# The first mixer in a fixed order by hand, with its gate summed by products

## The chip, the core and the metric

One Trainium2 chip; the kernel runs on one of its cores. The engines meant below: PE (matrix products; PEld is its weight load), DVE (vector work), ACT (activations and casts), POOL, and SP, which issues the loads. The time is device microseconds (us) of one execution; lower is better. The kernel before takes 1494.75 us in the median of three runs (1491.81 to 1494.77).

## The reference, cut to what matters

Two blocks of a transformer over 256 tokens of width 1024, batch 1, all in fp32. The change touches the mixer of the first block:

```python
mod = c_act @ w_ada + b_ada          # conditioning: 6 vectors of 1024
sh1, sc1, g1, sh2, sc2, g2 = split(mod)
h = x * (1 + sc1) + sh1
q, k, v, qi, ki, wi, gate_b, gate_c, hc = split(h @ w_in)
q, k, qi, ki = partial_rope(...)     # 8 heads of 64, k and v shared; 8 index heads of 32
rel = relu(einsum('bqhd,bsd->bqhs', qi, ki))
score = einsum('bqhs,bqh->bqs', rel, wi)       # causal
sel = top_k(score, 64)               # each query keeps 64 keys
attn = group_rms_norm(softmax(q k / 8 over sel) @ v, g)
u = gate_c * hc
conv = sum(conv_w[j] * u_pad[:, j:j + s] for j in range(3))
conv_out = group_rms_norm(gate_b * conv, g)
mix = concatenate([attn, conv_out]) @ w_out
x = layer_norm(ALPHA * x + g1 * mix, ln1_g, ln1_b)
```

After it come the first swiglu ffn (with sh2, sc2, g2) and a second block with four ffns, a differential attention and a gated recurrence; they are as before in both kernels.

## The kernel before, in words

Tokens are two tiles t of 128 rows. A product of two fp32 operands is done as three on values cut into a high and a low part (hi x hi, hi x lo, lo x hi). For weights ACT casts a loaded piece to its high part (L210, `whi`) and DVE subtracts it to get the low one (L223, `wlo`). `Stream` (`W`) holds that for all weights in order: `load_to` issues a load on SP, `highs_to` the casts, `split_to` the subtractions, `next` hands a piece of two halves over. Loaded pieces lie in five buffers `raw`, which the weights share with the loads of the conditioning matrix (`adaraw`, 1 MB each like a weight piece); a load starts when the buffer that it takes is free.

The conditioning vectors that follow the mixer (G1 its gate, SH2 and SC2 shift and scale of the ffn) are made from four loads each. DVE multiplies a loaded row block by the conditioning value of its partition and adds it to `adacc`, two operations a load (L558 the first, L560 the others). PE then sums `adacc` over partitions: for a gate by two products with ones, which leave the sum in all rows (L580), for a shift or scale by eight one-column products (L605); DVE adds the bias (`vcol`, L607).

`first_mixer` modulates and projects (`ps_att`, k loop over eight blocks of the width, with a third of the first two conv products `ps_c` in it), then the indexer (`ps_idx` L1271, relu on ACT, `score` L1277, eight rounds of MAX8 and MATCH_REPLACE8 for each tile, L1289 and L1291, then the mask `mb`), then eight attention units (tile t, four heads `quad`, parity e: logits `ps_lg` L1323, masked minimum L1333, exp L1337, transposes `ps_pt` L1345, weighted sum L1355), the head norm and its split into `mh`, `ml`. The other two conv products `ps_c` and two gate products `ps_gb` run in pieces between, followed by the taps (L1155, L1157), `gated` (L1163), a group norm `ps_gn` (L1440 to L1452) and the split of those features. `ps_wo` is the product with w_out; `finish` adds its last pieces, calls `between`, and does the residual (`u`, L261) and the norm.

What sets the order there: `order(False)` hands the mixer to a scheduler that takes the instructions by priority, and the table PLACES gives units, fills, splits, sums and norms their ranks. The rest of the kernel runs `order(True)`, as written.

Of the kernel before, what the change touches and what calls it, by code (L numbers as in the profile page):

```python
# [9 lines left out]
F32 = mybir.dt.float32  # L10
# [21 lines left out]

PLACES = {
# [7 lines left out]
}  # L41
# [383 lines left out]
class Net:  # L425
    def __init__(self, nc, tc, T, out, ctx, stop=None):
# [18 lines left out]
        self.ada_seq = [u for j in range(4) for u in (columns[2 * j], (G1, j), columns[2 * j + 1])]  # L445
# [7 lines left out]
        W.add([T["w_out"][j] for j in (2, 3, 0, 1)])  # L453
# [556 lines left out]
    def first_mixer(self):  # L1010
        nc, T, tc, W = self.nc, self.T, self.tc, self.W
        with ExitStack() as es:
# [3 lines left out]
            self.gate_bounds()  # L1016
            rope = m1.tile([P, 2, 32], F32, name="rope")
# [68 lines left out]
            def prepared(k):  # L1086

                if k == KT:
                    W.split_to(2 * W.at + 1)
# [15 lines left out]
            for k in range(KT):  # L1105
                W.load_to(k + 2)
                load(k + 3)
                if k == KT - 3:
                    nc.sync.dma_start(out=self.blk64, in_=T["k_blk64"])
                    nc.sync.dma_start(out=rope, in_=T["k_rope"])  # L1110
                    nc.sync.dma_start(out=causal, in_=T["k_causal"])
# [9 lines left out]
                if k != KT - 2:  # L1121
                    while thirds:
                        conv_third(*thirds.pop(0))
                parts = coming

            self.order(False)
            rank0 = tc.cur_priority

            def rank(name, default):

                n = PLACES.get(name, default)
                return tc.high_priority(offset=tc.cur_priority - rank0 - n)

            urgent = lambda: rank("chain", 0)

            late = []
            cw = self.col("conv_w")
            cv = m1.tile([P, 4, S], F32, name="cv", tag="cv")
# [4 lines left out]
            def some(n):  # L1143
                while late and n:
                    late.pop(0)()
                    n -= 1

            def conv_in(j, ps):
                with rank(f"cv{j}", 100 + 10 * j):
                    gc = self.w256("gc")  # L1150
                    u = m2.tile([P, S + 2], F32, name="cu")
                    nc.gpsimd.memset(u[:, 0:2], 0.0)
                    nc.scalar.copy(gc, ps[:, :S])
                    nc.vector.tensor_tensor(out=u[:, 2:], in0=ps[:, S:], in1=gc, op=ALU.mult)
                    nc.vector.tensor_scalar(out=cv[:, j], in0=u[:, 0:S], scalar1=cw[:, j:j + 1], scalar2=None, op0=ALU.mult)  # L1155
                    for d in (1, 2):
                        nc.vector.scalar_tensor_tensor(out=cv[:, j], in0=u[:, d:d + S], scalar=cw[:, 4 * d + j:4 * d + j + 1],  # L1157
                                                       in1=cv[:, j], op0=ALU.mult, op1=ALU.add)

            def gated(j, ps):  # L1160
                with rank(f"gb{j}", 200 + 10 * j):
                    y = cv[:, 2 * j:2 * j + 2].rearrange("p a b -> p (a b)")
                    nc.vector.tensor_tensor(out=y, in0=ps, in1=y, op=ALU.mult)  # L1163
                    sq = m2.tile([P, 2, 512], F32, name="gsq", tag="gsq")
                    nc.scalar.activation(sq[:, 0], y, AF.Square)
                    ys.append((y, sq))

            def normed(j):
                y, sq = ys[j]
                with rank(f"gn{j}", 220 + 10 * j):  # L1170
                    r = self.group_rstd(m1, sq, self.eps1)

                def rest():
                    with rank(f"nr{j}", 220 + 10 * j):
                        for a in range(2):
                            f = 4 + 2 * j + a
                            hf = self.w256("hfc")
                            g = m2.tile([P, 1], F32, name="cg")
                            nc.vector.tensor_scalar(out=g, in0=self.col("conv_g", 2 * j + a), scalar1=-0.5, scalar2=None, op0=ALU.mult)
                            nc.vector.scalar_tensor_tensor(out=hf, in0=y[:, a * S:(a + 1) * S], scalar=g, in1=r()[:, a * S:(a + 1) * S],  # L1180
                                                           op0=ALU.mult, op1=ALU.mult)
                            self.split(mh[:, f], ml[:, f], hf)
                return rest

            def product(name, q, done):
                with rank(f"split{q}", 500 + 50 * q):
                    parts = W.next(ahead=0, ada=False)
                ps = self.psum("acc", name)
                for n in range(2):
                    pieces = self.feat_pieces(ps, parts, n * S, n * P)  # L1190
                    for piece in range(2):
                        with rank(f"fill{q}", 500 + 50 * q):
                            next(pieces)
                        if n and piece:
                            done(ps)
                        yield

            def work():
                for j in (2, 3):
                    yield from product("ps_c", j - 2, lambda ps, j=j: late.append(lambda: conv_in(j, ps)))  # L1200
                for j in range(2):
                    yield from product("ps_gb", j + 2, lambda ps, j=j: late.append(lambda: gated(j, ps)))
                while len(ys) < 2:
                    some(1)
                rests = [normed(0), normed(1)]
                for j, r in enumerate(rests):
                    r()
                self.out_acc = self.rows_acc("ps_wo")
                for q, ks in ((4, (4, 5)), (5, (6, 7))):
                    with rank(f"split{q}", 500 + 50 * q):  # L1210
                        parts = W.next(ahead=0, ada=False)
                    for a, k in enumerate(ks):
                        for t in range(2):
                            with rank(f"fill{q}", 500 + 50 * q):
                                self.rows_mm(self.out_acc[t], parts[a], t, lhs(k), k == 4, False)
                            yield

            ys = []
            fill = work()
            filled = lambda n: [next(fill, None) for i in range(n)]  # L1220

            with urgent():

                pj = [m1.tile([P, 1024], F32, name=f"pj{t}", tag=f"pj{t}")[:, :ATT_COLS] for t in range(2)]
                for t in range(2):
                    nc.scalar.copy(pj[t][:, 512:], acc[t][1][:, :ATT_COLS - 512])
                for t in range(2):
                    nc.scalar.copy(pj[t][:, :512], acc[t][0])

                def rot(t, base, heads, dim):  # L1230
                    v = pj[t][:, base:base + heads * dim].rearrange("p (h d) -> p h d", h=heads)
                    c2 = rope[:, t:t + 1, 0:16].to_broadcast([P, heads, 16])
                    s2 = rope[:, t:t + 1, 16:32].to_broadcast([P, heads, 16])
                    sw = m2.tile([P, 9, 16], F32, name="sw")[:, :heads]
                    nc.vector.tensor_tensor(out=sw[:, :, 0:8], in0=v[:, :, 8:16], in1=s2[:, :, 0:8], op=ALU.mult)
                    nc.vector.tensor_tensor(out=sw[:, :, 8:16], in0=v[:, :, 0:8], in1=s2[:, :, 8:16], op=ALU.mult)
# [24 lines left out]
            for j in range(2):  # L1261
                conv_in(j, pcs[j])
# [600 lines left out]
```

## Time and profile before

| | before |
|---|---|
| time, median of 3 runs | 1494.75 us |
| lowest and highest | 1491.81, 1494.77 us |
| the profiled execution: time, span | 1493.31 us, 1491.5 us |
| PE busy | 1412.9 us (95%) |
| DVE busy | 1117.4 us (75%) |
| ACT busy | 720.1 us (48%) |
| POOL busy | 46.0 us (3%) |

The span is what the trace covers; the 1.8 us beside it belong to the execution's start and end. Busy shares are of the whole span; the mixer ends near 180 us of it.

### The profile page before, as it was taken

Reading aid. Unit: us, or ns where it says so; the run is one execution under the profiler, and the core shown is the slowest. Engines: PE = TensorE matmul, PEld = TensorE weight load, DVE = VectorE, ACT = ScalarE, POOL = GpSimd, SP = SyncE. Lnnn points to the kernel's source line nnn. Section 1 sums busy time; section 2 is a strip of 40 time slices with the busy share of each in tenths; the row PEclk is TensorE's granted clock in tenths of the full one; section 3 lists DMA queues with packets and bytes.
Section 4 is the critical chain, followed back from the end, with each engine's and each line's share of the span. In section 5 each row is a group of like instructions: output and inputs, shape, how many; then the busy total and the mean of one; then the engine's idle time right before and its main releaser. Section 6 shows DMA issues by size and latency. Waiting matters only on the chain.

```text
span 1491.5 us, 22826 instructions
## 1 busy us (share of the span) xinstructions
PE 1412.9 (95%) x9218; PEld 1270.9 (85%) x9218; DVE 1117.4 (75%) x1742; ACT 720.1 (48%) x1218; POOL 46.0 (3%) x45
## 2 busy tenths in 40 slices
PE   6987898999899999899999999999999899999998
PEld 5965787999799989677799998999997888799997
DVE  5877877876888867888886667876666998766545
ACT  5544343434443445556454445544445675544343
POOL 0001000000000000122100000000000000000000
PEclk9967999999999999999999999999999999999999
DMA  8925567878467878476567676486654334356650
GB/s 323 342 91 194 212 243 287 288 286 316 150 229 303 351 301 297 185 255 207 189 235 262 259 271 230 175 319 245 245 213 156 114 114 151 132 198 244 239 181 29
DMA packets 50346, 337.87 MB, mean 227 GB/s; under 512 B 5648, under 2 KB 7440, under 8 KB 11200
## 3 DMA queue, kind: packets, MB, share of 16 engines
q1 hardware_dynamic: 50096, 336.35, 61.2%
q8 instruction: 72, 1.18, 0.3%
q14 instruction: 34, 0.28, 0.1%
q10 hardware_dynamic: 144, 0.07, 0.0%
HBM read 335.33 MB, written 1.06 MB: 226 GB/s over the span
## 4 chain that ended last, share of the span: by engine, by line
PE 75%; DVE 14%; ACT 4%; issue 3%; POOL 2%; DMA 1%; SPq 0%; POOLq 0%; DVEq 0%; ACTq 0%
PE ps_dn L699 19%; PE ps_up L663 12%; PE ps_up L661 12%; PE ps_up L660 12%; DVE wlo L223 3%; PE ps_up L853 2%; DVE adacc L560 2%; PE ps_att L699 2%; PE ps_wo L699 1%; POOL qss L637 1%; PE ps_up L860 1%; ACT whi L210 1%; PE ps_do L699 1%; PE ps_g L699 1%; POOL oss L637 1%
## 5 line engine op out<-in xcount | busy, mean ns | idle before, releaser
L223 DVE TENSOR_TENSOR wlo<-raw,whi 128x1024 fp32r<-128x1024 f32 (+2 forms) x429 | 502.6, 1208 | 52.1 <-ACT whi L210 51.8
L210 ACT CAST whi<-raw 128x1024 fp32r<-128x1024 f32 (+2 forms) x429 | 427.8, 1038 | 138.7 <-issue 47.8
L661 PE MATMUL ps_up<-xh,wlo 128*128 128x256 f32 x1600 | 392.3, 283 | 3.8 <-DVE wlo L223 3.8
L660 PE MATMUL ps_up<-xh,whi 128*128 128x256 f32 x1600 | 393.6, 284 | 0.4 <-ACT whi L210 0.4
L661 PEld LDWEIGHTS ps_up<-xh,wlo 128*128 128x128 f32 x1600 | 306.1, 191 | 7.0 <-DVE wlo L223 4.4
L660 PEld LDWEIGHTS ps_up<-xh,whi 128*128 128x128 f32 x1600 | 305.8, 191 | 3.9 <-ACT g L950 0.9
L663 PE MATMUL ps_up<-xl,whi 128*128 128x256 f32 x1600 | 224.4, 283 | 0.0
L663 PEld LDWEIGHTS ps_up<-xl,whi 128*128 128x128 f32 x1600 | 206.2, 192 | 0.0
L560 DVE SCALAR_TENSOR_TENSOR adacc<-adaraw,cact,adacc 128x1024 f32<-128x1024 f32 x154 | 196.8, 1281 | 2.4
L950 ACT ACTIVATE g<-ps_up 128x256 f32<-128x256 f32 x100 | 38.5, 385 | 315.8 <-PE ps_up L663 315.8
L699 PE MATMUL ps_dn<-whi,hh 128*128 128x512 f32 x440 | 173.9, 395 | 0.0
L699 PE MATMUL ps_dn<-wlo,hh 128*128 128x512 f32 x440 | 172.8, 393 | 0.6 <-DVE wlo L223 0.6
L952 DVE TENSOR_TENSOR hu<-ps_up,g 128x256 f32<-128x256 f32 x100 | 42.3, 423 | 153.2 <-ACT g L950 153.0
L699 PE MATMUL ps_dn<-whi,hl 128*128 128x512 f32 x440 | 140.7, 394 | 0.0
L699 PEld LDWEIGHTS ps_dn<-whi,hl 128*128 128x128 f32 x440 | 82.6, 188 | 18.6
L699 PEld LDWEIGHTS ps_dn<-wlo,hh 128*128 128x128 f32 x440 | 82.8, 188 | 18.2 <-DVE wlo L223 1.0
L699 PEld LDWEIGHTS ps_dn<-whi,hh 128*128 128x128 f32 x440 | 83.1, 189 | 17.0 <-issue 0.2
L644 DVE TENSOR_TENSOR hl<-hu,hh 128x256 fp32r<-128x256 f32 x100 | 42.5, 425 | 47.3 <-ACT hh L643 47.3
L643 ACT CAST hh<-hu 128x256 fp32r<-128x256 f32 x100 | 40.7, 407 | 72.3 <-DVE hu L952 72.3
L637 POOL TENSOR_TENSOR rstd<-rstd,mhalf 128x1 f32<-128x1 f32 x16 | 8.7, 546 | 892.0 <-DVE rstd L313 642.1
L379 ACT ACTIVATE xh<-ps_tr,vcol,modA 128x128 fp32r<-128x128 f32 x48 | 18.1, 457 | 31.0 <-PE ps_tr L368 25.6
L1768 PE MATMUL ps_l<-hX 128*128 128x128 f32 x224 | 29.8, 276 | 0.6 <-DVE hX L1753 0.6
(357 smaller groups left out, 1947.9 us busy)
## 6 DMA issues: line engine op xcount, KB each, us to landing
raw<-in_up_dram SPq DMA_DIRECT2D x110, 1024.0 KB, 6.4
adaraw<-in_ada_dram SPq DMA_DIRECT2D x88, 1024.0 KB, 5.2
raw<-in_down_dram SPq DMA_DIRECT2D x55, 1024.0 KB, 6.6
adas<-in_ada_s_dram SPq DMA_DIRECT2D x8, 1024.0 KB, 5.4
raw<-in_w_qk_dram SPq DMA_DIRECT2D x8, 1024.0 KB, 7.2
raw<-in_w_att_dram SPq DMA_DIRECT2D x8, 724.0 KB, 6.6
raw<-in_w_conv_dram SPq DMA_DIRECT2D x4, 1024.0 KB, 8.0
raw<-in_w_out_dram SPq DMA_DIRECT2D x4, 1024.0 KB, 5.9
```

The source lines that it names most:

```text
L210: net.nc.scalar.copy(hi[:, :n], src)
L223: self.net.nc.vector.tensor_tensor(out=lo[:, :n], in0=src, in1=hi.bitcast(F32)[:, :n], op=ALU.subtract)
L560: nc.vector.scalar_tensor_tensor(out=acc, in0=raw[:, k], scalar=c[:, 2 * j + k:2 * j + k + 1], in1=acc, op0=ALU.mult, op1=ALU.add)
L637: self.nc.gpsimd.tensor_tensor(out=out, in0=in_, in1=self.mhalf[:, :n], op=ALU.pow)
L643: nc.scalar.copy(hi, src)
L644: nc.vector.tensor_tensor(out=lo, in0=src, in1=hi.bitcast(F32), op=ALU.subtract)
L660: mm(o, hi[:, at(k)], xh[:, k], start=k == 0, stop=False)
L661: mm(o, lo[:, at(k)], xh[:, k], start=False, stop=False)
L663: mm(o, parts[k // 4][0][:, at(k)], xl[:, k], start=False, stop=k == KT - 1)
L699: mm = lambda *args, **more: self.nc.tensor.matmul(*args, **more, **kw)
L950: self.last_silu = nc.scalar.activation(g, ps[:, :S], AF.Silu)
L952: nc.vector.tensor_tensor(out=u, in0=ps[:, S:], in1=g, op=ALU.mult)
```

## The change

The scheduler and its table go: `order(True)` holds for the whole mixer, and a sequence written by hand takes the place of the ranks. The first token tile goes ahead through rotation, indexer, scores and top-8 rounds; the eight units are pipelined (unit i's logits beside the weighted sum of unit i-2 and the transposes of i-1), and `filled(n)` puts n steps of `fills()` between them. G1 is no longer summed on DVE: `cb` holds the conditioning vector copied into 128 columns, and 16 fp32 products of the loaded rows with it give the gate in all rows at once. So G1's four loads come first, in the last two rounds of the projection. The products c2, c3, gb0 and gb1 come in six steps of eight products each. The first tap and the gains of the heads are on ACT (`scalar`), the taps wait until the units end, w_out is used in its own order (attention features first), the second tile's head split moves ahead of `between`, and `summed()` does DVE's two sums of one load. The group norm takes another PSUM pool and buffer.

```diff
-PLACES = {
-    "ada0": -54, "ada1": -129, "ada10": 1501, "ada11": 1295, "ada2": 1040, "ada3": 585, "ada4": 957,
...
-        self.ada_seq = [u for j in range(4) for u in (columns[2 * j], (G1, j), columns[2 * j + 1])]
+        self.ada_seq = [(G1, j) for j in range(4)] + columns
...
-        W.add([T["w_out"][j] for j in (2, 3, 0, 1)])
+        W.add(T["w_out"])
...
+            cb = m1.tile([P, KT, P], F32, name="cb", tag="cv")
+            nc.vector.tensor_copy(cb, self.cact[:, :KT, None].to_broadcast([P, KT, P]))
...
-                W.load_to(k + 2)
+                W.load_to(min(k + 2, KT - 1))
                 load(k + 3)
+                if k >= KT - 2:
+                    self.ada_load()
+                    self.ada_load()
...
-            self.order(False)
-            rank0 = tc.cur_priority
...
+            def sums():
+
+                pss = [self.psum("acc", "ps_gate") for a in range(2)]
+                for j in range(4):
+                    raw = self.ada_raw.pop(j)
+                    for k in range(2):
                         for a in range(2):
+                            nc.tensor.matmul(pss[a], cb[:, 2 * j + k], raw[:, k, a * 512:(a + 1) * 512], start=j == k == 0, stop=j == 3 and k == 1)
+                            yield
+                got["gate"] = pss
...
+            def fills():
+                yield from sums()
+                for name in ("ps_c2", "ps_c3", "ps_gb0", "ps_gb1"):
+                    yield from product(name)
...
+            for i in range(8):
+                logits(i)
+                if i == 4:
+                    chosen(1, 2)
+                    masked(1)
+                least(i)
+                if i >= 2:
+                    weighted(i - 2)
+                if i >= 1:
+                    turned(i - 1)
+                weights(i)
...
+                if i == 7:
+                    W.split_to(c2 + 3)
+                    filled(3)
+
+            weighted(6)
+            turned(7)
+            head_split(0)
+            conv_in(2, got.pop("ps_c2"))
+            filled(1)
+            weighted(7)
+            W.highs_to(c2 + 5)
+            rest[1] = head_norms(1)
...
+            ys = [gated(0)]
+            W.highs_to(c2 + 9)
+            summed()
+            W.split_to(c2 + 8)
+            filled(3)
+            norms.append(self.group_rstd(m1, ys[0][1], self.eps1))
...
+            normed(1, ys[1][0], norms[1]())
+            W.split_to(c2 + 11)
+            parts = W.next(ahead=0, loads=0, ada=False)
+            wo = [(p, k) for k, p in enumerate(parts, 2)]
+            W.load_to(c2 // 2 + 7)
+            self.ada_load()
+            self.ada_load()
+            summed()
+            for t in range(2):
+                for p, k in wo:
+                    self.rows_mm(out[t], p, t, lhs(k), False, False)
+            summed()
+            self.ada_load()
+
             def between():
-                head_split(1)
-                self.reduce_now(G1)
                 self.reduce_sums(SH2, "b")
                 self.reduce_sums(SC2, "t")
...
-            self.finish(self.out_acc, lhs, range(4), End(self, G1, 1.0, nxt, None, "ln"), between=between)
+            self.finish(out, lhs, range(4, 8), End(self, G1, 1.0, nxt, None, "ln"), between=between)
...
+            if scalar:
+                nc.scalar.activation(hf[:, k], src, AF.Copy, scale=gains[k])
+            else:
+                nc.vector.tensor_scalar(out=hf[:, k], in0=src, scalar1=gains[k], scalar2=None, op0=ALU.mult)
```

On PE the indexer products stand so in the kernel before (`ps_idx` the indexer, `ps_c` a conv product; the numbers of columns at the end):

```order
L675 MATMUL ps_c<-xl,whi 128x256
L1271 MATMUL ps_idx<-kiT,qiT 128x256
L1271 MATMUL ps_idx<-kiT,qiT 128x128
L1271 MATMUL ps_idx<-kiT,qiT 128x256
L1271 MATMUL ps_idx<-kiT,qiT 128x128
L673 MATMUL ps_c<-xh,whi 128x256
```

And so in the changed kernel, from the indexer to the first units (`ps_gate` the new sums, `ps_q` and `ps_k` the transposes for the heads):

```order
L1271 MATMUL ps_idx<-kiT,qiT 128x256 x4
L1172 MATMUL ps_gate<-adaraw,cb 128x512 x2
L1271 MATMUL ps_idx<-kiT,qiT 128x256 x4
L1172 MATMUL ps_gate<-adaraw,cb 128x512
L1257 MATMUL ps_q<-ident,pj_631 128x128 x4
L1260 MATMUL ps_k<-ident,kr_701 128x128
L1257 MATMUL ps_q<-ident,pj_632 128x128 x4
L1260 MATMUL ps_k<-ident,kr_708 128x128
L1172 MATMUL ps_gate<-adaraw,cb 128x512 x2
L1314 MATMUL ps_lg<-kT,qT 128x128 x2
```

The conv pieces have left the indexer and the first units, the gate sums stand in their place, and four indexer products in a row now belong to one tile and four heads, on different row strips.

On DVE the end of the mixer stands so before (L560 the sums, L223 the low parts, L1433 the second head split, L607 the reduced vectors, L261 the residual):

```order
L560 SCALAR_TENSOR_TENSOR adacc<-adaraw,cact,adacc 128x1024 x3
L223 TENSOR_TENSOR wlo<-raw,whi 128x1024 x4
L1430 TENSOR_SCALAR hf<-ps_at,cols 128x128 x4
L1433 TENSOR_TENSOR ml<-hf,mh 128x4x128
L589 TENSOR_TENSOR gate<-ps_red,gate 128x512 x2
L607 TENSOR_TENSOR vcol<-ps_red,cols 128x8 x2
L223 TENSOR_TENSOR wlo<-raw,whi 128x1024
```

And in the changed kernel (all line numbers ten lower, L550 and L548 the sums, L213 the low parts, L597 the reduced vectors):

```order
L213 TENSOR_TENSOR wlo<-raw,whi 128x1024
L550 SCALAR_TENSOR_TENSOR adacc<-adaraw,cact,adacc 128x1024 x4
L213 TENSOR_TENSOR wlo<-raw,whi 128x1024 x5
L597 TENSOR_TENSOR vcol<-ps_red,cols 128x8
L548 TENSOR_SCALAR adacc<-adaraw,cact 128x1024
L550 SCALAR_TENSOR_TENSOR adacc<-adaraw,cact,adacc 128x1024 x7
L597 TENSOR_TENSOR vcol<-ps_red,cols 128x8
L213 TENSOR_TENSOR wlo<-raw,whi 128x1024
```

All eight sums of SC2 now stand behind five splits, the fifth of which is the first ffn weight's, and behind SH2's reduced vector; the head split and the gate's additions have gone from here.

## Rows read from the trace of the kernel before

**Rows 1.** Stretches of the mixer: length, busy us of each engine, granted clock, DMA share, GB/s.

```profile
core 0: us, PE busy (x) PEld busy (x) DVE busy (x) ACT busy (x) POOL busy (x), PEclk, DMA share, GB/s
62.40:74.00 11.60, 11.60 (x89) 10.98 (x89) 10.83 (x28) 5.87 (x12) 0.20 (x2) 1.00 0.83 303
74.00:88.00 14.00, 14.00 (x52) 11.89 (x51) 11.30 (x32) 5.30 (x10) 0.00 (x0) 0.52 0.45 166
...
97.00:103.00 6.00, 1.10 (x7) 0.67 (x6) 6.00 (x30) 3.42 (x8) 0.00 (x0) 0.91 0.00 0
...
134.00:172.70 38.70, 26.65 (x116) 20.82 (x116) 31.77 (x48) 13.15 (x19) 1.82 (x1) 0.83 0.61 217
```

**Rows 2.** Timeline of PE: start, duration, operation, count, idle time before and its releaser.

```profile
102.38 0.47 PE L1345 MATMUL ps_pt<-ident,lg 128*128 128x128 f32 x1 [4.90 <-ACT lg L1337]
...
132.93 1.16 PE L1355 MATMUL ps_pt<-pj,pT 128*128 128x128 f32 x8 [0.73 <-ACT pT L1348]
142.90 2.08 PE L1440 MATMUL ps_gn<-gsq,blk 128*128 128x512 f32 x2 [8.80 <-ACT gsq L1165]
```

**Rows 3.** Timeline of all engines at the mixer's end.

```profile
166.16 1.88 PE L580 MATMUL ps_red<-adacc,ones 128*128 128x512 f32 x4
...
167.87 4.74 PE L605 MATMUL ps_red<-ones,adacc 128*128 128x1 f32 x32
...
172.66 0.17 DVE L607 TENSOR_TENSOR vcol<-ps_red,cols 128x8 f32<-128x8 f32 x1 [2.52 <-PE ps_red L605]
...
173.87 1.28 DVE L261 SCALAR_TENSOR_TENSOR u<-ps_wo,gate 128x512 f32<-128x512 f32 x2
```

**Rows 4.** Timeline of PE, products like those that move or come.

```profile
71.52 1.57 PE L1271 MATMUL ps_idx<-kiT,qiT 32*128 32x256 f32 x8
...
93.91 0.71 PE L1323 MATMUL ps_lg<-kT,qT 64*128 64x128 f32 x8
...
120.48 1.13 PE L1323 MATMUL ps_lg<-kT,qT 64*128 64x256 f32 x4
121.54 0.66 PE L1345 MATMUL ps_pt<-ident,lg 128*128 128x128 f32 x4
121.95 0.36 PE L675 MATMUL ps_gb<-xl,whi 128*128 128x256 f32 x1
...
122.51 0.28 PE L673 MATMUL ps_gb<-xh,whi 128*128 128x256 f32 x1
122.62 0.28 PE L674 MATMUL ps_gb<-xh,wlo 128*128 128x256 f32 x1
122.87 1.16 PE L1355 MATMUL ps_pt<-pj,pT 128*128 128x128 f32 x8
123.78 0.36 PE L675 MATMUL ps_gb<-xl,whi 128*128 128x256 f32 x1
...
652.53 1.14 PE L1573 MATMUL ps_s<-kn,qn 64*128 64x256 f32 x8
```

**Rows 5.** Timeline of DVE: weight splits, a 512-column row, sums of loads.

```profile
109.93 3.49 DVE L223 TENSOR_TENSOR wlo<-raw,whi 128x1024 fp32r<-128x1024 f32 x3
...
133.96 0.68 DVE L1447 TENSOR_TENSOR gsq<-gsq,gr 128x512 f32<-128x512 f32 x1
...
143.97 6.06 DVE L560 SCALAR_TENSOR_TENSOR adacc<-adaraw,cact,adacc 128x1024 f32<-128x1024 f32 x5
```

**Rows 6.** Timeline of ACT: square, the norm's first step, weight casts, four gains.

```profile
142.22 0.63 ACT L1165 ACTIVATE gsq<-cv 128x512 f32<-128x512 f32 x1 [1.91 <-DVE cv L1163]
145.01 0.69 ACT L1442 ACTIVATE gsq<-ps_gn,eps 128x512 f32<-128x512 f32 x1 [2.17 <-PE ps_gn L1440]
...
150.31 1.99 ACT L210 CAST whi<-raw 128x1024 fp32r<-128x1024 f32 x2 [2.62 <-PE ps_wo L699]
...
180.83 1.51 ACT L379 ACTIVATE xh<-ps_tr,modB,modA 128x128 fp32r<-128x128 f32 x4 [0.98 <-PE ps_tr L368]
```

**Rows 7.** Timeline of POOL: the two powers of the head norms.

```profile
121.42 2.62 POOL L637 TENSOR_TENSOR ss<-ss,mhalf 128x8 f32<-128x8 f32 x1 [48.14 <-DVE ss L1368]
136.53 1.82 POOL L637 TENSOR_TENSOR ss<-ss,mhalf 128x8 f32<-128x8 f32 x1 [12.49 <-DVE ss L1368]
```

**Rows 8.** Tile adaraw from 40 to 215 us: its loads from issue to landing.

```profile
DMA to landing us min/median/max: 4.7/4.9/7.5
```

More of the change, by code (lines that the diff above doesn't have):

```diff
@@ L1141, in first_mixer @@
             lhs = lambda k: (mh[:, k], ml[:, k])
[L1143 to L1146, printed above, removed]
+            cus = {}
             def conv_in(j, ps):
[L1149 to L1158, printed above, removed]
@@ L1185, in product @@
[L1185 to L1188, printed above, removed]
-                for n in range(2):
[L1190 to L1195, printed above, removed]
-                        yield
@@ L1198, in work @@
[L1198 to L1216, printed above, removed]
@@ new lines, in gated, with normed @@
+            def gated(j):
+                y = got["cv"][:, 2 * j:2 * j + 2].rearrange("p a b -> p (a b)")
+                nc.vector.tensor_tensor(out=y, in0=got.pop(f"ps_gb{j}"), in1=y, op=ALU.mult)
+                sq = m2.tile([P, 2, 512], F32, name="gsq", tag="gsq")
+                nc.scalar.activation(sq[:, 0], y, AF.Square)
+                return y, sq
+            def normed(j, y, r):
+                for a in range(2):
+                    f = 4 + 2 * j + a
+                    hf = self.w256("hfc")
+                    g = m2.tile([P, 1], F32, name="cg")
+                    nc.vector.tensor_scalar(out=g, in0=self.col("conv_g", 2 * j + a), scalar1=-0.5, scalar2=None, op0=ALU.mult)
+                    nc.vector.scalar_tensor_tensor(out=hf, in0=y[:, a * S:(a + 1) * S], scalar=g, in1=r[:, a * S:(a + 1) * S],
+                                                   op0=ALU.mult, op1=ALU.mult)
+                    self.split(mh[:, f], ml[:, f], hf)
@@ new lines, in product, with part @@
+            def product(name):
+                mm = nc.tensor.matmul
+                g = 2 * W.at
+                W.highs_to(g + 1)
+                hi = [W.parts[g + i][0] for i in range(2)]
+                ps = self.psum("acc", "ps_c" if "c" in name else "ps_gb")
+                at = lambda k, n: slice(k % 4 * 2 * P + n * P, k % 4 * 2 * P + (n + 1) * P)
+                def part(ws, x, n, first, last):
+                    for k in range(KT):
+                        mm(ps[:, n * S:(n + 1) * S], ws[k // 4][:, at(k, n)], x[:, k], start=first and k == 0, stop=last and k == KT - 1,
+                           skip_group_check=True)
+                for n in range(2):
+                    for x in (xh, xl):
+                        part(hi, x, n, n == 0 and x is xh, False)
+                        yield
+                lo = [w[1] for w in W.next(ahead=0, loads=0, ada=False)]
+                for n in range(2):
+                    part(lo, xh, n, False, n == 1)
+                    if n:
+                        got[name] = ps
+                    yield
@@ L1304, in first_mixer @@
[L1304 to L1315 removed]
+                        nc.vector.scalar_tensor_tensor(out=scores[t], in0=rel[:, e], scalar=wi[:, t, h:h + 1],
+                                                       in1=causal[:, S - n:] if g == e == 0 else scores[t], op0=ALU.mult, op1=ALU.add)
@@ new lines, in chosen, with masked @@
+            def chosen(t, rounds):
+                for r in range(rounds):
+                    best = m2.tile([P, 8], F32, name="best", tag=f"best{t}")
+                    nc.vector.max(out=best, in_=scores[t])
+                    nc.vector.match_replace(out=scores[t], in_to_replace=best, in_values=scores[t], imm_value=GONE)
+            mb = {}
+            def masked(t):
+                n = (t + 1) * P
+                bias = mb[t] = m1.tile([P, n], F32, name=f"mb{t}")
+                nc.vector.tensor_scalar(out=bias, in0=scores[t], scalar1=-2e38, scalar2=NEG, op0=ALU.is_gt, op1=ALU.mult)
+                nc.vector.tensor_tensor(out=bias, in0=bias, in1=causal[:, S - n:], op=ALU.add)
@@ L1317, in logits @@
+            at, sm, pss, lgs, pts = {}, {}, {}, {}, {}
+            units = [(t, quad, e) for t in range(2) for quad in range(2) for e in range(2)]
+            def logits(i):
+                t, quad, e = units[i]
                 n = (t + 1) * P
@@ L1389, in first_mixer @@
-            for i, u in enumerate(units):
-                with rank(f"unit{i}", i):
-                    ps = logits(*u)
-                    lg = weights(*u, ps)
-                    pt, pT = turned(u[0], lg)
-                    weighted(u[0], pt, pT)
-                    keep(*u, pt)
-                if i % 4 == 3:
-                    with rank(f"norm{u[0]}", 10 + 10 * u[0]):
-                        head_norms(u[0])()
-                if i == 6:
-                    with rank("hs0", 12):
-                        head_split(0)
-                some(2)
-                filled(2)
-                ada(self.ada_loaded - 1)
-                for n in range(min(2 - i % 2, 12 - self.ada_loaded)):
-                    self.ada_load()
@@ L1407, in first_mixer, with gate_rows @@
-            for _ in fill:
-                some(1)
-            some(len(late))
-            ada(self.ada_loaded)
-            tc.cur_priority = rank0 + 5000
+                self.gain_split(ps, t, [self.col("attn_g", k) for k in range(4)], mh, ml, 0, True)
+            def gate_rows():
+                g = self.vecs[G1]
+                for a, ps in enumerate(got.pop("gate")):
+                    sl = slice(a * 512, (a + 1) * 512)
+                    nc.vector.tensor_tensor(out=g[:, sl], in0=ps, in1=g[:, sl], op=ALU.add)
@@ new lines, in summed @@
+            def summed(n=1):
+                self.ada_to(self.ada_done + n)
+            c2 = 2 * W.at
+            copied(0)
+            index_rows(0)
+            conv_third(*thirds.pop(0))
+            copied(1)
+            index_turned(0)
+            index_rows(1)
+            conv_third(*thirds.pop(0))
+            index_turned(1)
+            head_rows(0)
+            head_rows(1)
+            for j in range(2):
+                conv_in(j, pcs[j])
+            for i in range(W.at, W.at + 2):
+                W.load_to(i)
@@ new lines, in first_mixer @@
+            W.load_to(c2 // 2 + 6)
+            ys.append(gated(1))
+            self.out_acc = out = self.rows_acc("ps_wo")
+            parts = W.next(ahead=0, loads=0, ada=False)
+            wo = [(p, k) for k, p in enumerate(parts)]
+            for p, k in wo:
+                self.rows_mm(out[0], p, 0, lhs(k), k == 0, False)
+            normed(0, ys[0][0], norms[0]())
+            norms.append(self.group_rstd(m1, ys[1][1], self.eps1))
+            W.highs_to(c2 + 11)
+            summed()
@@ new lines, in first_mixer @@
+            W.split_to(c2 + 10)
+            for p, k in wo:
+                self.rows_mm(out[1], p, 1, lhs(k), k == 0, False)
+            normed(1, ys[1][0], norms[1]())
+            W.split_to(c2 + 11)
+            parts = W.next(ahead=0, loads=0, ada=False)
+            wo = [(p, k) for k, p in enumerate(parts, 2)]
+            W.load_to(c2 // 2 + 7)
+            self.ada_load()
+            self.ada_load()
+            summed()
+            for t in range(2):
+                for p, k in wo:
+                    self.rows_mm(out[t], p, t, lhs(k), False, False)
```

327 lines of the change are left out of this document (176 added, 151 removed), and 6 rows, old and new, of the table PLACES.

## The prediction

> **What bounds the kernel now.** I read the page's busy times first: PE works for nearly the whole span, so time can come back only where PE waits or runs slowly. Then the stretches of the first mixer [rows 1], since the order changes nowhere else. From 74 to 88 PE is busy for all 14.00 us, at a granted clock of 0.52; from 97 to 103 it works 1.10 of 6.00 us while DVE works all of them; from 134 to 172.7 it works 26.65 of 38.70 us, DVE 31.77. So the mixer is bound by PE at the lower clock, then by DVE twice. The two long waits of PE are in [rows 2]: 4.90 us before the first transposed unit at 102.38 (DVE runs the top-8 rounds and the masks until then), and 8.80 us before 142.90, behind the last weighted sum of attention (132.93 + 1.16 = 134.1). Last I read who ends the mixer [rows 3]: PE's 32 small reductions for SH2 and SC2 from 167.87, DVE's second vcol at 172.66, then the residual u at 173.87. The mark for the change is this second vcol: what follows it (24 products for the second token tile, the norm, the first ffn) stands in the same order in both kernels.
>
> **What changes, and the sum.** It has three parts: up to the first indexer products, a stretch that PE sets, and a tail that DVE sets.
>
> *Up to 62.4* nothing on the path moves: the projection's k loop is as it was. The new copy cb is one DVE operation at the start, where DVE waits for data anyway; I cost it at nothing, and at 0.6 if that cover were gone. The four G1 loads now come ahead of four weight loads; from 97 to 103 the kernel before moves nothing [rows 1], so I cost them at nothing unless a load comes late (below).
>
> *PE's stretch*, from 62.4 to the transposes of unit 7 (prices from [rows 4]):
> - Indexer products: 8 groups a kernel. A pass of four instructions (two of 256 and two of 128 columns) took 1.57 us at the full clock on one row strip (71.52). After the change neighbours sit on different strips. What that gives is seen at 652.53, where eight records of the diff attention on alternating strips took 1.14, as long as four did on one strip (120.48, 1.13). So half of 5.2: **2.6**, or 5.2 if they don't overlap.
> - Gate sums: 16 fp32 products of 128x512. The two of the old reduce took from 166.16 to 167.87 [rows 3], 0.86 each: **13.8**. For it DVE loses eight sums of about 1.2 (five took 6.06 at 143.97 [rows 5]), the first at 0.7, so 9, and PE loses the 1.7 of the old reduce, which was late in the stage.
> - Ten transposes for the heads at 0.11: **1.1**. Logits: four units of the second tile at 1.06 (120.48 to 121.54), four of the first at 0.35 (eight records for two units in 0.71, 93.91): **5.6**. Transposes of the units at 0.41 (121.54 to 121.95), half for the first tile: **2.5**. Weighted sums up to unit 6, at 0.91 (122.87 to 123.78) and 0.45: **4.5**.
> - Fills that the hand order puts there: product c2, 48 of 0.12 from start to start (122.51 to 122.62): **5.8**, and the first half of c3: **2.9**.
> - Hand-offs: small-row and fp32 groups now alternate with wide products some 24 times; each such step costs 0.13 more than the product's own 0.12 (122.62 to 122.87): **3.1**. Waits for the second tile's copies: **1.1**.
>
> Together 43, so the stretch ends at **105.4**. The kernel before ends its units at 134.1: the change is some 28 us ahead here. But before, three of four conv products were done by then; now half of c3 and both gb are still to come, with their splits and the sums for SH2 and SC2.
>
> *The tail* ping-pongs between ACT and DVE, each in order [rows 5 to 7]. A DVE row of 512 columns takes .6 to .7 from start to start (0.68 at 133.96, the next 0.60 later), a square .63:
> 1. Transposes of the first tile .5; ACT gains 1.45 (four 0.36 apart, 180.83), casts, copies and square, together 5.75; DVE .8; the power on POOL 2.2 (1.82 here, 2.62 for the other tile; I take the middle); scaling .65, transposes .5; ACT gains and cast 2.05, two weight casts 2.0 (150.31), first tap .35: 14.8, to 120.2. The gains moved to ACT cost it 3 us here; on DVE they cost 2.4.
> 2. Taps .8, two weight splits 2.3 (1.15 each, 109.93), gated .7; then ACT has square .6, two casts 2.0 and the four norm steps 2.65 (145.01), while DVE's next row waits for them: 9.05, to 129.25.
> 3. DVE .7, split 1.15, gated .65, .65, two splits of features with their casts 2.7: 135.1. The second norm chain, queued on ACT behind those casts, ends at 137.35.
> 4. .65, the second A5 sums 2.4, split 1.15, .6, 2.8, split 1.15: 146.1.
> 5. Four sums of A6 and A7 4.8, four splits of the last w_out pieces 4.6: 155.5.
> 6. The fifth split in the same DVE run belongs to the first ffn weight. Its load waits for the buffer that the fourth split frees: .1 + 4.9 of landing (the median of the adaraw loads, which are as large [rows 8]) + cast 1.05 + split 1.15. Behind it, in order on DVE: vcol .2, then all eight sums of SC2, 9.05. Then PE's 16 reductions 2.4 (half of the 32 of 167.87, at the clock they had): 18.85, to 174.35, and the second vcol starts at **174.5**.
>
> Before it started at 172.66: **+1.8 us**. On the profiled execution's 1493.31 (span 1491.5 and 1.8 around it) that is 1495.1; that execution lies 1.44 under the median of the runs, so against the median 1494.75 the forecast is **1496.5 us**. DVE works only some 45 of the tail's 69 us; the rest is waiting in order, and that is where the 28 us of lead go back.
>
> Bounds: indexer without overlap +2.6; landing at 7.5 instead of 4.9 +2.6; POOL at either end ±.4; hand-offs at nothing −3.1; reductions at the full clock −1.2. Together 1492 to 1502 around the forecast.
>
> A rule speaks against the alternation: the Trainium skill, "TensorEngine Tiling (Array Packing)", Key Properties, says that changing the tiling mode drains TensorE, while different tiles may run in parallel. The trace shows both as small: 0.13 at the step [rows 4], and the pair at 652.53. With the page alone a drain has no price; by the row it is the 3.1 already in the sum.
>
> **The rivals.**
> *Clock falls in PE's stretch (slower).* From 74 to 88 PE was busy throughout and yet ran at 0.52 [rows 1], after indexer passes on single strips. In the new stretch indexer, logits and single-weight fp32 products follow each other for 20 us. If the lower clock is granted from 62 to 90 for half of it, the 28 us there hold 14 more: 1510. Against it: the passes use several strips at once, the gate sums use all rows, and the full clock lasted from 62.4 to 74 under a mix. It decides if the mean clock over 62 to 105 is under 0.8. The Trainium skill, "TensorE: Matmul & The Clock Gate", Part 1, says that activity releases the throttle; by that a busy PE stays fast and the rival is void, but 74 to 88 disagrees, with PE busy in 14.00 of 14.00 us.
> *Waits fall away in the tail (faster).* I let ACT and DVE wait for each other at eleven places, 24 us in all. If ACT's casts run ahead and the norm chains start as soon as their products end, half goes: 12 us less, 1484.5. For it: before, DVE worked 31.77 of 38.70 us in its own tail [rows 1]. Against it: both queues are in order, and a norm's reader stands ahead of ready splits. It decides if DVE waits under 16 us from 105 to 174.
> *Loads late and no overlap (slower).* Both upper bounds: 1502. The first weight load of the ffn and four A loads share the queue in step 6.
> *The change does less than it says:* if PE's stretch ended at 115, the tail would move with it, 1506; this I count with the first rival.
>
> **How the numbers follow.** A difference under 0.2%, 3.0 us, can't be told from no change here. The sum holds: 0.47, of it 0.26 within 0.2%, 0.15 slower (above 1497.7), 0.06 faster. Clock rival 0.20, late loads 0.08, both slower. Shorter tail 0.25, faster. So faster 0.31, same 0.26, slower 0.43. The range for 8 in 10 reaches into both rivals: 1482 leaves out the lower part of the shorter tail, 1512 the worse clock; 1492 to 1502 is the likeliest case's own.
>
> **What would show it.** Right: unit 7's transposes near 105; gate sums 0.86 apart; PE idle some 15 us between 137 and 172; the DVE row before the fifth split waiting near 6 us for ACT; eight sums of SC2 in one run before the second vcol at 174. Wrong: a clock near 0.5 between 62 and 90; the norm readers on DVE waiting under 1 us; SC2's sums done before 160; or the ffn starting other than 7 to 8 us after the second vcol.

## The result, and the profile after

| | before | after |
|---|---|---|
| median (lowest, highest; runs) | 1493.28 us (1491.07, 1494.77; 4) | 1501.47 us (1501.15, 1502.20; 4) |
| ratio, 95% interval | | 1.0057 [1.0039, 1.0074] |
| the profiled execution: time, span | 1493.31 us, 1491.5 us | 1501.15 us, 1499.4 us |
| PE, DVE, ACT busy | 1412.9, 1117.4, 720.1 us | 1413.0, 1113.9, 724.0 us |

The change costs 8.2 us. (The kernel before ran a fourth time here, so its median is 1493.28 and not 1494.75.) Each engine is busy for as long as before within 4 us; the time went into waits.

The stretches of the changed kernel, against [rows 1] (same columns):

```profile
62.40:74.00 11.60, 11.02 (x50) 5.63 (x50) 8.86 (x36) 5.14 (x13) 0.00 (x0) 1.00 0.30 100
74.00:88.00 14.00, 14.00 (x56) 7.43 (x55) 11.42 (x44) 6.42 (x23) 0.00 (x0) 1.00 0.47 157
97.00:103.00 6.00, 6.00 (x47) 5.48 (x47) 4.68 (x16) 5.17 (x13) 1.70 (x2) 1.00 0.10 42
103.00:134.00 31.00, 26.08 (x178) 23.26 (x177) 19.34 (x29) 16.44 (x33) 2.61 (x2) 0.94 0.43 150
134.00:172.70 38.70, 19.60 (x76) 14.65 (x74) 26.88 (x32) 11.62 (x16) 0.00 (x0) 0.72 0.57 215
```

To 103 the change does what it says: from 97 to 103 PE is busy for all 6.00 us instead of 1.10, and the granted clock of 74 to 88 is 1.00 (2.4 GHz) instead of 0.52 (1.2 GHz for nearly all of it). In the last stretch both lose: PE works 19.60 us instead of 26.65, DVE 26.88 instead of 31.77. On PE, in the timeline against [rows 4], the indexer, a gate pair, a unit, and the transposes of unit 7:

```profile
63.49 0.71 PE L1271 MATMUL ps_idx<-kiT,qiT 32*128 32x128 f32 x8
64.13 1.98 PE L1172 MATMUL ps_gate<-adaraw,cb 128*128 128x512 f32 x4
66.04 1.13 PE L1271 MATMUL ps_idx<-kiT,qiT 32*128 32x256 f32 x8
67.11 1.98 PE L1172 MATMUL ps_gate<-adaraw,cb 128*128 128x512 f32 x4
...
94.33 1.13 PE L1314 MATMUL ps_lg<-kT,qT 64*128 64x256 f32 x4
95.39 1.16 PE L1354 MATMUL ps_pt<-pj,pT 128*128 128x128 f32 x8
...
105.07 0.60 PE L1342 MATMUL ps_pt<-ident,lg 128*128 128x128 f32 x4
```

The end of the mixer, in the timeline of DVE, against [rows 3]: the last sums of SH2, four weight splits, the ffn weight's split, SC2's sums, and the second vcol.

```profile
146.68 5.24 DVE L550 SCALAR_TENSOR_TENSOR adacc<-adaraw,cact,adacc 128x1024 f32<-128x1024 f32 x4
151.84 4.63 DVE L213 TENSOR_TENSOR wlo<-raw,whi 128x1024 fp32r<-128x1024 f32 x4
164.30 1.22 DVE L213 TENSOR_TENSOR wlo<-raw,whi 128x1024 fp32r<-128x1024 f32 x1 [7.83 <-ACT whi L200]
165.44 0.16 DVE L597 TENSOR_TENSOR vcol<-ps_red,cols 128x8 f32<-128x8 f32 x1
165.52 0.74 DVE L548 TENSOR_SCALAR adacc<-adaraw,cact 128x1024 f32<-128x1024 f32 x1
166.29 9.21 DVE L550 SCALAR_TENSOR_TENSOR adacc<-adaraw,cact,adacc 128x1024 f32<-128x1024 f32 x7
179.17 0.17 DVE L597 TENSOR_TENSOR vcol<-ps_red,cols 128x8 f32<-128x8 f32 x1 [3.66 <-PE ps_red L595]
```

DVE waits 7.83 us for a cast whose load was issued only at 156.50, when the fourth split had ended:

```profile
156.50 14.08 SPq L186 DMA_DIRECT2D raw<-in_up_dram  x3
```

and ten us of sums (165.52 to 175.50), whose data needn't wait for that weight, stand behind it. Then PE's reductions, which waited for the sums:

```profile
158.56 1.84 PE L595 MATMUL ps_red<-ones,adacc 128*128 128x1 f32 x16
175.56 3.57 PE L595 MATMUL ps_red<-ones,adacc 128*128 128x1 f32 x16 [15.16 <-DVE adacc L550]
178.99 0.77 PE L689 MATMUL ps_wo<-whi,mh 128*128 128x512 f32 x1
```

The same sixteen records take 1.84 us for SH2 and 3.57 for SC2 after a wait of 15.16. The second vcol starts 6.5 us later than the 172.66 of [rows 3]; the span is 7.9 us longer.

### The profile page after: what moved, and what is told of

Same layout as the page of the kernel before. It is cut to its first block, busy times and chain, and to the rows that moved or that the text cites. A ratio compares the mean times of both kernels' runs of the same rounds, so it can differ in the third digit from the quotient of the medians.

```text
span 1499.4 us, 22882 instructions
## 1 busy us (share of the span) xinstructions
PE 1413.0 (94%) x9246; PEld 1266.1 (84%) x9246; DVE 1113.9 (74%) x1723; ACT 724.0 (48%) x1230; POOL 45.9 (3%) x45
## 3 DMA queue, kind: packets, MB, share of 16 engines
HBM read 335.33 MB, written 1.06 MB: 224 GB/s over the span
## 4 chain that ended last, share of the span: by engine, by line
PE 74%; DVE 14%; ACT 5%; issue 3%; POOL 2%; DMA 2%; SPq 0%; POOLq 0%; DVEq 0%; ACTq 0%
PE ps_dn L689 18%; PE ps_up L653 12%; PE ps_up L651 12%; PE ps_up L650 12%; DVE wlo L213 4%; PE ps_up L843 2%; DVE adacc L550 2%; PE ps_att L689 2%; ACT whi L200 1%; POOL qss L627 1%; PE ps_up L850 1%; PE ps_g L689 1%; PE ps_gate L1172 1%; PE ps_do L689 1%; DMA raw<-in_up_dram 1%
## 5 line engine op out<-in xcount | busy, mean ns | idle before, releaser
L213 DVE TENSOR_TENSOR wlo<-raw,whi 128x1024 fp32r<-128x1024 f32 (+2 forms) x429 | 502.7, 1208 | 57.0 <-ACT whi L200 56.7
L550 DVE SCALAR_TENSOR_TENSOR adacc<-adaraw,cact,adacc 128x1024 f32<-128x1024 f32 x147 | 188.5, 1282 | 2.8
## 6 DMA issues: line engine op xcount, KB each, us to landing
raw<-in_w_att_dram SPq DMA_DIRECT2D x8, 724.0 KB, 6.4
```

What stands on the lines that cost most here:

```text
L213: self.net.nc.vector.tensor_tensor(out=lo[:, :n], in0=src, in1=hi.bitcast(F32)[:, :n], op=ALU.subtract)
L550: nc.vector.scalar_tensor_tensor(out=acc, in0=raw[:, k], scalar=c[:, 2 * j + k:2 * j + k + 1], in1=acc, op0=ALU.mult, op1=ALU.add)
```

## The experiments

Three theories on the loss. 1: the end of the mixer is a queue on DVE, and the order of that queue costs the time. 2: the 16 gate products on PE cost it. 3: PE's half clock after its wait costs it.

All runs are edits of the changed kernel behind its projection. Even so its first indexer products start at 60.91 to 63.09 us in the profiled executions (61.09 after the change). Where a time of one trace is held against that of another, I say what is left when this start is taken off.

**Sums first.** SC2's sums ahead of the ffn weight's split, in `finish`:

```diff
         if between is not None:
+            self.ada_finish(SC2)
             W.split_to(2 * W.at)
             between()
```

> The changed kernel with one move: the eight sums of SC2 stand ahead of the first ffn weight's split on DVE instead of behind it. Theory 1 (the end of the mixer is a queue on DVE: the split waits for a load that starts only when the fourth split has ended, and the sums wait behind it): the sums start at 156.4 instead of 165.5, the second vcol comes near 170 instead of 179.2, the time falls by 8 to 9.5 us to 1492 to 1494. Theory 2 (the 16 gate products on PE made the mixer longer): the path lies ahead of this place, the time stays within 2 us of 1501.5. Theory 3 (PE waits so long that it runs at half clock at the end): PE still waits some 6 us there, so at most 2 us come back.

Measured: 1492.62 us, ratio to before 0.9998 [0.9985, 1.0010]. The whole loss comes back. DVE's timeline, the four splits and what follows:

```profile
153.29 4.62 DVE L213 TENSOR_TENSOR wlo<-raw,whi 128x1024 fp32r<-128x1024 f32 x4
157.83 0.75 DVE L548 TENSOR_SCALAR adacc<-adaraw,cact 128x1024 f32<-128x1024 f32 x1
158.61 9.21 DVE L550 SCALAR_TENSOR_TENSOR adacc<-adaraw,cact,adacc 128x1024 f32<-128x1024 f32 x7
167.74 1.22 DVE L213 TENSOR_TENSOR wlo<-raw,whi 128x1024 fp32r<-128x1024 f32 x1
...
171.49 0.17 DVE L597 TENSOR_TENSOR vcol<-ps_red,cols 128x8 f32<-128x8 f32 x1 [2.46 <-PE ps_red L595]
```

The sums now cover the landing and the cast of the ffn weight, and the 7.83 us are gone. The second vcol comes 7.7 us earlier than after the change, 9.4 with the start (62.78) taken off. Theory 1 holds, as the main cause; 2 can't explain it.

**Gate on DVE.** The eight sums of G1 back on DVE, two products with ones, no gate products:

```diff
-                pss = [self.psum("acc", "ps_gate") for a in range(2)]
...
+                for n in range(16):
+                    if n >= 8 and n % 2 == 0:
+                        summed()
                     yield
...
-                g = self.vecs[G1]
...
+                r = self.reduce(G1, "acc")
+                r(0)
+                r(1)
...
-            self.ada_done = 4
```

> The changed kernel with G1 summed on DVE again (eight operations, at units 0 to 3) and two products with ones in place of the 16 gate products; the order is otherwise kept. Theory 1: DVE is busy some 33 of the 43 us of PE's stretch and gets 9 more, so the stretch ends between 101 and 106 instead of 105; all behind it moves by as much: 1497 to 1502. Theory 2: the 13.8 us less on PE come back nearly whole: 1488 to 1491. Theory 3: no change at the end, 1500 to 1502.

Measured: 1511.91 us, 1.0128 [1.0109, 1.0146], ten us slower than the changed kernel; outside what any theory gave. The stretch from 62.4 to 103, first after the change, then here:

```profile
62.40:103.00 40.60, 40.02 (x214) 26.49 (x214) 32.64 (x115) 22.10 (x63) 1.70 (x2) 1.00 0.38 133
```

```profile
62.40:103.00 40.60, 30.83 (x122) 21.41 (x120) 37.73 (x112) 16.54 (x52) 0.00 (x0) 0.62 0.37 130
```

DVE is busy for 37.73 of 40.60 us, PE for 30.83 at a clock of 0.62, and the first head's transposes start at 116.39 instead of 105.50, 8.9 us later with the start (63.09) taken off. The sums stand on DVE between the minima of the units, and the units wait for them: of its idle time from 62 to 120 PE spends 8.1 us in five waits for ACT's exponentials (L1329), which need those minima, and none on a load. So theory 2 is wrong in sign: in this order the gate products are worth ten us. Whether DVE's load or PE's clock makes them so, a later run tells.

**Gains on DVE.** The gains of the heads' split as before the change:

```diff
-                self.gain_split(ps, t, [self.col("attn_g", k) for k in range(4)], mh, ml, 0, True)
+                self.gain_split(ps, t, [self.col("attn_g", k) for k in range(4)], mh, ml, 0)
```

> The changed kernel with the eight gains of the two head splits on DVE again, as before the change. Theory 1: ACT loses 1.1 us ahead of the square of the second tile, where DVE waits from 104.6 to 108, so the tail moves by about 1 us: 1500 to 1501.5. Theory 2 and 3: nothing. If the gains had cost the 3 us that I counted on ACT for them, 1498.5.

Measured: 1503.0 us, 1.0071 [1.0055, 1.0087]; above the 1500 to 1501.5 that I had expected, but its interval overlaps that of the change, so the times do not tell them apart. In the trace the second split's gains come behind the taps on DVE (118.51), and the second vcol at 182.36, 3.2 us later, of which 1.1 were there before the gains. So by this one trace the gains cost some 2 us more on DVE than on ACT, where I had expected 1 less.

**Warm.** 64 products between the two reductions:

```diff
                 self.reduce_sums(SH2, "b")
+                ps = self.psum("b", "ps_warm")
+                for n in range(64):
+                    nc.tensor.matmul(ps, mh[:, n % 8, 0:P], mh[:, 0:2].rearrange("p a b -> p (a b)"), start=n == 0, stop=n == 63)
                 self.reduce_sums(SC2, "t")
```

> The changed kernel with 64 products of 512 columns into a buffer that nobody reads, on PE between the reductions of SH2 and SC2, where PE waits from 160.4 to 175.6; the outputs do not depend on them. Theory 3: PE stays at the full clock, SC2's reductions take 1.84 instead of 3.57 and the 24 products behind them 5.6 instead of 8.4: 1.7 us on the vcol, 1.7 to 4.5 on the time, 1497 to 1500. Theory 1 alone: the vcol moves by the 1.7 us of the reductions and no more, 1499.5 to 1500. If the clock does not matter there: 1501.5.

Measured: 1500.07 us, 1.0047 [1.0032, 1.0062]; the interval overlaps that of the change. The trace shows what the median only hints at: the reductions take

```profile
175.47 1.95 PE L595 MATMUL ps_red<-ones,adacc 128*128 128x1 f32 x16 [0.28 <-DVE adacc L550]
```

instead of 3.57, and the vcol comes at 177.46, 1.7 us earlier. Theory 3 is right for a small part: the medians differ by 1.4 us, just under the least that it gave, 1.7.

**Gate on DVE, PE kept busy.** The gate on DVE as above, with 16 products of the gate's form that nobody reads:

```diff
+                ps = self.psum("acc", "ps_gate")
                 for n in range(16):
                     if n >= 8 and n % 2 == 0:
                         summed()
+                    nc.tensor.matmul(ps, cb[:, n % 8], self.x[:, 0, :512], start=n == 0, stop=n == 15)
                     yield
```

> G1 summed on DVE as in the run with the gate on DVE (1511.9 us), and in the places of the 16 gate products 16 products of the same form whose result nobody reads; the outputs do not depend on them. What made that run slow by 10 us is open: either DVE's eight sums between the units' minima (then PE's extra work can't help: 1510 to 1515), or PE's half clock from 74 to 97, which PE had there because it waited (then the clock is back at 1.00 and half or more of the 10 us return: 1502 to 1507).

Measured: 1515.02 us, 1.0139 [1.0124, 1.0153]. The clock is back and the time is not:

```profile
62.40:103.00 40.60, 33.95 (x143) 18.58 (x143) 35.10 (x103) 14.80 (x47) 0.00 (x0) 0.94 0.33 120
```

PE has the work of the changed kernel here, at nearly its clock, and the first head's transposes still start at 118.43, 11.8 us later than after the change with the start (62.18) taken off. So it is DVE's load between the units that cost the ten us, not PE's clock.

**Sums first and warm.** 26 such products in the kernel with the sums first:

```diff
             self.ada_finish(SC2)
...
                 self.reduce_sums(SH2, "b")
+                ps = self.psum("b", "ps_warm")
+                for n in range(26):
+                    nc.tensor.matmul(ps, mh[:, n % 8, 0:P], mh[:, 0:2].rearrange("p a b -> p (a b)"), start=n == 0, stop=n == 25)
                 self.reduce_sums(SC2, "t")
```

> SC2's sums ahead of the ffn weight's split (1492.6 us), and 26 products that nobody reads on PE between the reductions of SH2 and SC2, where PE waited 6.02 us and then ran at half clock; the outputs do not depend on them. If the half clock costs there: SC2's reductions 1.84 instead of 3.58 and 12 products of .43 at .23 behind them, 1.7 to 3 us, 1489.5 to 1491. If not: 1492 to 1493.

Measured: 1492.12 us, 0.9990 [0.9980, 1.0000]. The reductions fall from 3.58 to 1.95 us and the vcol comes at 168.67 instead of 171.49, of which 1.6 us are left with the starts (61.53, 62.78) taken off. But the medians of the two kernels differ by 0.5 us: inconclusive for the time.

**Sums early.** Sums first, and two pairs of sums moved into waits of DVE; each later `summed()` takes the load after:

```diff
             turned(7)
+            summed()
             head_split(0)
...
+            summed()
             norms.append(self.group_rstd(m1, ys[0][1], self.eps1))
```

> SC2's sums ahead of the ffn weight's split (1492.6 us), and besides two of DVE's pairs of sums moved into waits of DVE in the tail: one pair ahead of the first head split (DVE waited 3.34 us for ACT there), one ahead of the first group norm's result (2.57 us). Theory 1 (the tail is a queue on DVE with waits in it, in which any sum that fits a wait is free): each pair of 2.6 us leaves the stretch in which DVE never waits, 146 to 171; the vcol comes 4 to 5 us earlier, 1487.5 to 1489. If loads land too late for the earlier places or if the tail is bound by ACT and PE: 1491 to 1494.

Measured: 1487.54 us, 0.9955 [0.9943, 0.9968]; a second time, on another chip, 1487.84 us, 0.9969 [0.9951, 0.9988]. DVE's timeline at the two places and at the end:

```profile
104.43 0.75 DVE L548 TENSOR_SCALAR adacc<-adaraw,cact 128x1024 f32<-128x1024 f32 x1
105.21 1.28 DVE L550 SCALAR_TENSOR_TENSOR adacc<-adaraw,cact,adacc 128x1024 f32<-128x1024 f32 x1
107.85 0.69 DVE L1556 TENSOR_TENSOR ml<-hf,mh 128x512 fp32r<-128x512 f32 x1 [1.35 <-ACT mh L1555]
...
127.29 2.60 DVE L550 SCALAR_TENSOR_TENSOR adacc<-adaraw,cact,adacc 128x1024 f32<-128x1024 f32 x2
129.81 0.68 DVE L1570 TENSOR_TENSOR gsq<-gsq,gr 128x512 f32<-128x512 f32 x1
...
164.96 0.17 DVE L597 TENSOR_TENSOR vcol<-ps_red,cols 128x8 f32<-128x8 f32 x1 [2.45 <-PE ps_red L595]
```

The split behind the first pair starts where it did (108.03 after the change, 107.85 here), the norm behind the second 0.2 us later (129.59, 129.81): the sums are all but free there. The vcol is 6.5 us earlier than with the sums first alone; 1.9 of that are the start (60.91 against 62.78), and the 4.7 left are the length of the two pairs, 4.6. It is 14 us earlier than after the change.

**One strip.** The indexer's products of a group in the order strip, strip's second, next strip:

```diff
-                for e in range(2):
-                    for g in gs:
+                for g in gs:
+                    for e in range(2):
                         nc.tensor.matmul(pss[g][:, e], qiT[32 * g:32 * g + 32, t, e], kiT[32 * g:32 * g + 32, :n], start=True,
                                         stop=True, tile_position=(32 * g, 0))
```

> The changed kernel (1501.5 us) with the indexer's four products of a group ordered so that two on one row strip follow each other. If neighbours on different strips overlap as I counted, eight pairs lose some of it: the products take 1.5 to 2.6 us more and the tail moves with them, 1503 to 1504. If the overlap is not worth it or does not reach the path: 1501 to 1502.

Measured: 1502.66 us, 1.0051 [1.0037, 1.0064], the changed kernel's ratio within its interval. The four of 256 columns still take what they took:

```profile
67.09 1.14 PE L1271 MATMUL ps_idx<-kiT,qiT 32*128 32x256 f32 x8
```

(1.07 from their start to the next gate product in both kernels). My expectation fell: a second product on the same strip in between costs nothing. The overlap over a group of two strips stays in either order; a whole group on one strip was not run.

**Real work.** The kernel with the sums early, and six of the 24 last w_out products between the two reductions:

```diff
-            between()
+            between(lambda: [self.rows_mm([acc[1][0]], p, 1, lhs(k), False, False, 0) for p, k in pk[:2]])
...
-            for p, k in pk:
+            for p, k in pk[2 if a == 0 and between is not None else 0:]:
...
-            def between():
+            def between(some):
                 self.reduce_sums(SH2, "b")
+                some()
```

> The best version so far (sums in DVE's waits and ahead of the ffn weight's split, 1487.5 us, second vcol at 165.0) with six of the 24 products of the second token tile moved between the reductions of SH2 and SC2, where PE waited 1.27 us and then ran at half clock until 171. If PE's wait brings the half clock: SC2's reductions take 1.9 instead of 3.6 and the products behind run at .23, the vcol comes 1.5 us earlier and the first transposes 2 us earlier, 1485 to 1486.5. If the clock falls whatever PE does there (the one-column reductions themselves): 1487 to 1488.5.

> The same kernel as the run with the sums moved early, beside the one with real work between the reductions, so that the two are compared on one chip: 1486.5 to 1488.5.

Measured on one chip: 1486.67 us, 0.9964 [0.9947, 0.9981], against 1487.84 us for the kernel with the sums early; it falls between the two ranges that I had set. The reductions take 1.84 us and the vcol comes at 163.70:

```profile
161.82 1.84 PE L595 MATMUL ps_red<-ones,adacc 128*128 128x1 f32 x16
163.70 0.17 DVE L597 TENSOR_TENSOR vcol<-ps_red,cols 128x8 f32<-128x8 f32 x1 [0.89 <-PE ps_red L595]
170.95 1.46 PE L358 MATMUL ps_tr<-ident,u 128*128 128x128 f32 x8 [3.03 <-ACT u L315]
```

The clock's part at the vcol is 1.4 to 1.6 us, against the two traces with the sums early (164.96 and 166.27, starts 60.91 and 62.36; here 61.22); the medians differ by 1.2 us, less than either interval is wide. PE then waits 3.03 us for the norm, which is now what ends last. The times show that both of these versions beat both kernels, the one before by 5 to 7 us and the changed one by some 14; they don't rank the two.

## Why the prediction was right in its side and short in its size

The forecast was 1496.5 us, slower by 1.8, which by the prediction's own 3.0 us can't be told from no change; it is slower by 8.2, inside the range, at the upper edge of the likeliest case's own. That the 1501.47 lie beside the 1502 of late loads without overlap is luck: the overlap held, and the load gave 1.7 of the 2.6 us that this rival needs from it.

**PE's stretch** was forecast to end at 105.4; the transposes of unit 7 start at 105.07 and end by 105.5. That this agrees so well is in part luck: the first indexer products start at 61.09 and not 62.4, and the stretch is 1.4 us longer than the 43. Single terms were off by up to 1.2 us:

- Groups of four indexer products took 0.64 and 1.07 (63.49 to 64.13, 66.04 to 67.11), 3.4 in all instead of 2.6. The overlap was right, but the 5.2 that I halved was low: four passes of 1.57 make 6.3.
- Four gate records with their hand-off took 1.91 (64.13 to 66.04), 0.95 a product, where I had 0.86 and the hand-off apart.
- Logits of the second tile took 1.06 as forecast, those of the first 0.64 (74.75 to 75.39) and not 0.35: my price came from two units together (93.91), and here each stands alone.
- The 0.13 of a hand-off was read between two groups of 128 rows (122.62 to 122.87). The step to 64 rows in the same trace is 0.21 (120.27 to 120.48) against the product's 0.12, so 0.09.
- PE waited less, 0.58 of 40.60 us.

**The clock rival is void**: 1.00 from 62.4 to 103, with PE nearly always busy. The rule of the Trainium skill, "TensorE: Matmul & The Clock Gate", Part 1, that activity releases the throttle, gives this stretch, and the 0.62 of the run in which PE waited for DVE; it still doesn't give the 0.52 of a busy PE in [rows 1].

**The tail to the fourth split** came out step by step: first tap done at 120.0 (forecast 120.2), first norm's reader at 129.6 (129.25), its features split at 135.6 (135.1), second reader at 137.7 (137.35), 146.7 (146.1), fourth split ended at 156.5 (155.5). So the lead of 28 us did go back in the waits of the two queues. The rival of a shorter tail did not come: from 105 to the fourth split DVE waited some 15 us, for the first head's cast, the two norms and smaller steps, and from 105 to 174 it waited 23, over the 16 that the prediction had set for it.

**Step 6 was mis-sized**, with the mechanism right: 18.85 us forecast, 22.7 measured. The load took from 156.50 until the cast at 163.22, 6.7 us and not 5.0; I had taken the median landing, and two other loads were still to land when it was issued. The eight sums took 10.0 us, 1.3 each and not 1.2. The reductions took 3.66 instead of 2.4: I halved the 4.74 of [rows 3] as if it were all at one clock, and it is 1.00 there until 170 and 0.50 from 171 on. Sixteen take 1.84 at the one and 3.57 at the other, so neither my 2.4 nor my 1.2 for the full clock is a price at one clock, and I had PE idle for 15 us ahead of mine. With 1.0 us from the steps before, that makes the 4.7 us between 174.5 and 179.17.

**Behind the vcol** I forecast nothing. The half clock lasts until 184.7 there, 5.5 us after the vcol (4.2 before), and the first transposes come 8.2 us after it instead of 7.5, just outside the 7 to 8 that the prediction had named as a sign of being wrong. That is 0.7 us of the 7.9 by which the span grew; of the last 0.7, in the first ffn, the cause was not tested.

What the runs add to the argument: the whole loss hangs on one place in DVE's queue. That SC2's sums stand behind a split which waits for a load costs 8.9 us (sums first). Of the parts that I had weighed as costs, the gate products save 10.4 us in this order. The heads' gains on ACT save some 2 us by one trace; the times don't show it.

## What to carry to other kernels

In a queue that runs in order, look at what stands behind the instruction that waits for the latest load: work whose data is already there belongs ahead of it, and fits a wait further up if it is no longer than the wait. When the queue of one engine is what the units wait for, moving 9 us off it can be worth more than the 14 us that the move costs an engine with time to spare; here it was worth ten. A lead won early shows nothing until the last chain is followed: the mark to compare is the instruction behind which both orders are the same.

## What the runs showed that I had not expected

PE's clock fell although its wait was short: with the sums early PE waited 1.27 us between the reductions of SH2 and SC2, and those of SC2 took 3.57 us at a granted clock of 0.50; with six products in that gap they took 1.84 at 1.00.

```profile
161.35 3.57 PE L595 MATMUL ps_red<-ones,adacc 128*128 128x1 f32 x16 [1.27 <-DVE adacc L550]
```

In a second execution the wait was 0.89 us and the reductions took 3.43. The kernel before shows it without any wait: PE works without a gap from 163 to 178, from 167.87 to 172.48 on the 32 one-column records of [rows 3], and the clock is 1.00 from 169 to 170, 0.58 from there to 171 and 0.50 from 171 to 176. So a wait of PE is not needed for the half clock at this place, and the kernel before pays for it too. What the one-column records themselves do to it was not tried.
